# An mLSTM and window-attention decoder layer on one core: the first output gates beside the sample attention, sample states in half tiles, and other steps moved

## The chip, the cores and the metric

The kernel runs on one core of a Trainium2 chip. The metric is device time in microseconds (us), the median of several runs. A profiled execution gives the trace; its line numbers are those of the kernel before. Engines are called PE (TensorE, matrix products), DVE (VectorE), ACT (ScalarE), POOL (GpSimd) and SP (SyncE, which issues most of the DMAs from a queue in order).

## The reference

One layer of a hybrid decoder is applied to a prompt (512 tokens) and to 8 samples of 4 tokens, which come with a state. All data are float32.

```python
u = x @ w_in                                   # 2048 -> 18952 columns
q_m,k_m,v_m,o_m,z_m, q_a,k_a,v_a,z_a, g_m,g_a, i_pre,f_pre = split(u)
# mLSTM, 4 heads of 512; per chunk, with carry (C, n, m)
s    = (q @ k.T) * d                           # d: decays of the gates
num  = s @ v + inter * (q @ C);  den = sum(s) + inter * (q @ n)
h_m  = num / max(|den|, exp(-m_row))
C    = decay * C + (w * k).T @ v               # samples: C is (8, 4, 512, 512), read and written
# attention over a window of 128, 32 heads of 64, 4 kv heads, ALiBi, sinks
h_a  = softmax([q_a @ k_a.T / 8 - slope * dist, sink]) @ v_a
# merge
br_m = layernorm(h_m) * mlstm_norm_w * sigmoid(o_m) * silu(z_m)
br_a = h_a * silu(z_a)
y    = sigmoid(g_m) * (br_m @ w_proj_m) + sigmoid(g_a) * (br_a @ w_proj_a)
out  = layernorm(2**0.25 * x + y @ w_out)
```

It returns the outputs of prompt and samples, the mLSTM states C, n, m of both, and the last 128 keys and values of both.

## The kernel before

All 544 tokens (512 of the prompt, then 32 of the samples) go through one set of products. A float32 factor is split into a high part `wh` (rounded to the type of the fast product) and a rest `wl` (`split`, L177 to L184: a copy on ACT, a subtraction on DVE), and a product is the sum of three.

*First columns.* `gemm` multiplies the columns of the attention's values (two tiles of 128) and keys (two tiles) in the plain way, with `gates_product` after the first. `attn_values` and `attn_keys` transpose the results and store them. Beside them `x_sums` forms sums of quarters of x on POOL, DVE and ACT, which the next stage needs.

*Pairs.* `paired` goes over 72 pairs of 128 columns of `w_in`. By a scheme of Strassen's kind a pair is seven half products (`half_product`, L568 and L570, 24 matmuls of 272 columns each) instead of eight. `prepare` adds and splits weights up to three half products ahead, under a priority of `AHEAD` = 400; `gather` takes the results out of PSUM into the tiles O1 and O2 (pool `ev`, three buffers). At the end of a pair, `w["end"]` handles its two column tiles. The first 35 pairs (marked `acc`, they let a DMA do some of the additions) hold the 16 pairs of attention queries and their gates (`end_qz`), with other columns between. Then come, for the mLSTM heads 0 to 3, four pairs of output gates each (`end_oz`), heads 2 and 3 having six pairs of v, k and q ahead of theirs, and nine pairs of merge gates.

*Side work.* Generators in `live` are advanced by `tick()`, one step each; a pair calls it after the half products 0, 1, 3, 4 and 6. Two matter here. `attentions` does the prompt's attention for each pair of queries in 12 steps, then the attention of the samples (`sample_attention`), then opens the pools of the sample states (`open_samples`) and sets `state["samples"]`. `samples` takes mLSTM heads from `chain_` (a head enters when its last output-gate pair has ended) and runs `sample_head`: `sample_prep`, then for each of 8 batches a load of the state C (1 MB, `load_C`, L915), four or three steps, four matmuls with C (L1033), four updates (L1037, L1038) and two stores (L1040), then `sample_finish`. `until(cond)` calls `tick()` until a condition holds, with no product between; `end_qz(k)` uses it to let the attention of the pair before end, and `end_oz` to let the sample attention end:

```python
def end_oz(k):
    def end(o, z_):
        until(lambda: state["samples"])
        sg = st1([128, T], "sz", p="pz")
```

The tile `sz` comes from the pool `pz`, which `open_samples` opens.

*Order.* The program order gives each instruction a priority (a block under `tc.high_priority(offset=n)` counts as n instructions earlier). A scheduler in the framework then orders every engine's queue, DMA queues too, by these priorities and by its own model of the times, and sets all semaphores. On the chip each queue runs in that order. Tiles with the same tag in a pool share its buffers.

*Rest.* After the pairs, products with `w_proj_a`, beside the prompt's mLSTM cells, then with `w_proj_m` and `w_out`, and the layer norm.

The functions that the change touches, and those that call them:

Of the kernel before, what the change touches and what calls it, by code (L numbers as in the profile page):

```python
# [73 lines left out]
def _build(tc, nc, i, o, es):  # L74
# [123 lines left out]
    def mm():  # L198
        return psA.tile([128, 2, 512], F32, tag="mm", name=nm("mm"))

    def gemm(wv, c0, xh, xl, cols=EVEN, raws=(None, None), every=8):
        ps = mm()
        for half in range(2):
            raw = raws[half] or load_half(wv, c0, half)
            wh, wl = split(raw)
            products(ps, half, wh, wl, xh, xl, cols, every)
        return ps

# [271 lines left out]
    def last_sum(s4):  # L480

        for ch in range(4):
# [7 lines left out]
            hilo(r12, s4[0][:, ks_], s4[1][:, ks_])  # L490
            yield

    for kk in range(2):
        ps = gemm(win, VA_ + kk * 128, xh, xl, raws=((raw0[0], raw0[1]), (raw0[2], None))[kk], every=4)
        if kk == 0:
            spawn(x_sums())
            gates_ps = gates_product()
        vt = ev()
        A.copy(two(vt[:]), pv(ps))
        attn_values(kk, vt)  # L500
    for kk in range(2):
        ps = gemm(win, KA + kk * 128, xh, xl, every=4)
        kt = ev()
        A.copy(two(kt[:]), pv(ps))
        attn_keys(kk, kt)
    drain()
    for src, dst in ((d_ks, kb_s), (d_vr[SEQ:T], vb_s)):
        nc.sync.dma_start(dst[:, 124:128].rearrange("b t k d -> b t (k d)"), src.rearrange("(b t) c -> b t c", t=NTS))
# [93 lines left out]
    def paired(work, first=iter(())):  # L602

        steps = [(w, n) for w in work for n in range(7)]
        ready = 0
        load_a(work[0])
        load_b(work[0])
        for at, (w, n) in enumerate(steps):

            while ready < min(at + 3, len(steps)):  # L610
                with tc.high_priority(offset=AHEAD):
                    prepare(*steps[ready])
                ready += 1
            p = at // 7 + 1
            if p < len(work):
                if n == 3:
                    load_a(work[p])
                elif n == 4:
                    load_b(work[p])
            half_product(w, n)  # L620
            with tc.high_priority(offset=AHEAD):
                gather(w, n)
            next(first, None)
            if n == 6:
                w["end"](w["O1"], w["O2"])
            if n in (0, 1, 3, 4, 6):
                tick()


# [100 lines left out]
    def end_qz(k):  # L730

        def end(o1, o2):
            until(lambda: state["open"] and state["done"] == k)
            qs = []
            for a in range(2):
                q = btile("bq", [128, T], "q", F32R)
                own, oth = slice(a * 64, a * 64 + 64), slice(64 - a * 64, 128 - a * 64)
                A.activation(q[own], o1[own], AF.Copy, scale=-0.125)
                V.scalar_tensor_tensor(q[oth], o1[own], -0.125, r32(q[own]), op0=ALU.mult, op1=ALU.subtract)
                qs.append(q)  # L740
            nc.sync.dma_start(d_qa[k], o1[:, SEQ:T])
            sz = btile("b1", [128, T], "sz")
            A.activation(sz[:], o2[:], AF.Sigmoid)
            V.tensor_tensor(out=sz[:], in0=o2[:], in1=sz[:], op=ALU.mult)
            nc.sync.dma_start(d_bra[k][:, SEQ:T], sz[:, SEQ:T])
            waiting[k] = (qs, sz)
        return end

    def attentions():
        while gates_ in live:  # L750
            yield
        for _ in last:
            pass
        esG.close()
        open_attention()
        state["open"] = True
        for k in range(16):
            if k % 4 == 0:
                kv = kv_head(k // 4)
            while k not in waiting:  # L760
                yield
            yield
            yield from attention(k, *waiting.pop(k), kv)
            state["done"] = k + 1
        esB.close()
        yield from sample_attention()
        esT.close()
        open_samples()
        state["samples"] = True
# [2 lines left out]
    esT = ExitStack()  # L772

    def sample_attention():
        t1, t2 = pool(esT, "t1", 1), pool(esT, "t2", 2)
        gas = t1.tile([128, 16, NS], F32, name="gas")
        qraw = t1.tile([128, 2, GRP, NS], F32, name="qraw")
        qas = t1.tile([128, 2, NB, GRP, NTS], F32, name="qas")
# [72 lines left out]
        for b in range(NB):  # L851
            if b % 2 == 0:
                PTs = []
                for bb in range(2):
                    pt = sm()
                    PE.transpose(pt[:, 0:128], E[:, b + bb, 0:128], ident)
                    PE.transpose(pt[:32, 128:256], En[:, b + bb], ident)
                    PT = t2.tile([128, 256], F32, tag=f"PT{bb}", name=nm("PT"))
                    A.copy(PT[:, 0:128], pt[:, 0:128])
                    V.tensor_copy(PT[:32, 128:256], pt[:32, 128:256])  # L860
                    PTs.append(PT)
                yield
                yield
            PT = PTs[b % 2]
            for kvh in range(KVH):
                dst = po[(kvh % 2) * 64:(kvh % 2) * 64 + 64, (kvh // 2) * 256 + b * 32:(kvh // 2) * 256 + b * 32 + 32]
                tp = (0, (kvh % 2) * 64)
                PE.matmul(dst, vb[:, b, kvh * 64:kvh * 64 + 64], PT[:, kvh * 32:kvh * 32 + 32], start=True, stop=False, tile_position=tp)
                PE.matmul(dst, vas[:, kvh * 64:kvh * 64 + 64], PT[:32, 128 + kvh * 32:160 + kvh * 32], start=False, stop=True, tile_position=tp)
# [31 lines left out]
    sp = {}  # L901

    def open_samples():
        for name, bufs in (("s1p", 1), ("sC", 2), ("sw", 2), ("pz", 1)):
            sp[name] = pool(esS, name, bufs)

    def st1(shape, tag, dt=F32, p="s1p"):
# [3 lines left out]
        return sp["sw"].tile([128, 512], F32, tag="w", name=nm("w"))  # L911

    def load_C(h, b):
        ct = sp["sC"].tile([128, 4, 512], F32, tag="C", name=nm("C"))
        nc.sync.dma_start(ct[:], i["state_mlstm_C"][b, h].rearrange("(c p) v -> p c v", p=128))  # L915
        return ct

    def sample_prep(h, r):
        qs = st1([128, 4, NS], "qs", p="sw")
# [91 lines left out]
    def sample_head(h):  # L1011
        r = {}
        nxt = load_C(h, 0)
        yield from sample_prep(h, r)
        pC = None
        for b in range(NB):
            ct = nxt
            if b + 1 < NB:
                nxt = load_C(h, b + 1)

            qz = st1([128, 4, NS], "qz", p="sw")
            G.memset(qz[:], 0.0)
            G.tensor_copy(qz[:, :, b * 4:b * 4 + 4], r["qs"][:, :, b * 4:b * 4 + 4])
            Ab = st1([128, 512], "Ab", F32R)
            G.tensor_scalar(Ab[:], r32(r["kA"][:]), cc[:, C_M8 + b:C_M8 + b + 1], None, op0=ALU.mult)
            for _ in range(4 - b % 2):
                yield
            if b == 0:
                pC = sm()

            with tc.high_priority(offset=3000):
                for c in range(4):
                    PE.matmul(pC[c * 32:c * 32 + 32, :], qz[:, c], ct[:, c],  # L1033
                              start=(b == 0), stop=(b == NB - 1), tile_position=(0, c * 32))
            for c in range(4):
                pu = sm()
                PE.matmul(pu[:], Ab[:, c * 128:c * 128 + 128], r["V4"][:], start=True, stop=True)  # L1037
                V.scalar_tensor_tensor(ct[:, c], ct[:, c], dcb[:, h, b:b + 1], pu[:], op0=ALU.mult, op1=ALU.add)  # L1038
                if c % 2:
                    nc.sync.dma_start(C_s[b, h, (c - 1) * 128:c * 128 + 128, :].rearrange("(c p) v -> p c v", p=128),  # L1040
                                      ct[:, c - 1:c + 1])
        yield from sample_finish(h, r, pC)

    chain_ = []
# [1 line left out]

    def samples():
        while True:
            if not chain_:
                yield  # L1050
                continue
            h = chain_.pop(0)
            if h is None:
                break
            yield from sample_head(h)

        esS.close()
        pf = pool(esF, "pf", PF)
        for k in range(PF):
            st = pf.tile([128, T], F32, tag="pf", name=nm("pf"))  # L1060
            nc.sync.dma_start(st[:], d_bra[k])
            ahead.append(st)
# [10 lines left out]

    def end_oz(k):
        def end(o, z_):
            until(lambda: state["samples"])
            sg = st1([128, T], "sz", p="pz")
            A.activation(sg[:], z_[:], AF.Sigmoid)
            A.activation(o[:], o[:], AF.Sigmoid)
            V.scalar_tensor_tensor(sg[:], z_[:], wn[:, k:k + 1], sg[:], op0=ALU.mult, op1=ALU.mult)  # L1080
            G.tensor_tensor(out=sg[:], in0=sg[:], in1=o[:], op=ALU.mult)
            nc.sync.dma_start(d_g[k], sg[:])
# [38 lines left out]
            work.append(fill.pop(0))  # L1121
    for w in work:
        w["acc"] = True
    for h in range(MH):
        if h >= 2:
            work += vkq(h)
# [418 lines left out]
```

## Time and profile before

| | us |
|---|---|
| median of 3 runs | 2616.19 |
| lowest and highest | 2612.90, 2619.99 |
| the profiled execution | 2613.4 |
| its span in the trace | 2611.5 |
| PE busy | 2544.5 (97%) |
| DVE, ACT, POOL busy | 1694.6, 1178.1, 350.7 |
| mean granted clock of PE | 0.989 |

The trace covers 2611.5 of the profiled execution's 2613.4 us. The granted clock is 1.00 where PE runs at full speed. "A <- B" in a list of waits reads: A's engine sat idle before A until B had ended; a name with q (SPq) is an engine's queue of DMA issues. A matmul's duration is longer than the distance between the starts of two that follow each other, since they are pipelined.

### The profile page before, as it was taken

What the parts mean: (1) busy time and instruction counts of PE and PEld (TensorE: products, weight loads), DVE (VectorE), ACT (ScalarE), POOL (GpSimd) and SP (SyncE); (2) the same over time, 40 slices, a digit from 0 to 9 for tenths busy, and PEclk for the clock granted to TensorE, in tenths of its full rate; (3) what the DMA queues carried; (4) which work ended last, traced back from release to release, by engine and by line L of the source; (5) the groups of instructions that cost most, each with busy time, mean ns of one, the idle gap of its engine ahead of it and who ended that gap; (6) DMA issues with size and microseconds to landing.
All of it is one profiled execution on the core that took longest, in us unless ns stands there. A gap on an engine that the chain in (4) does not pass through costs nothing.

```text
span 2611.5 us, 48884 instructions
## 1 busy us (share of the span) xinstructions
PE 2544.5 (97%) x19970; PEld 2468.1 (95%) x19970; DVE 1694.6 (65%) x2508; ACT 1178.1 (45%) x1908; POOL 350.7 (13%) x334
## 2 busy tenths in 40 slices
PE   8999999999999998999999999999999999999997
PEld 7999999999999997989899899899999999999997
DVE  7867776676676673877778777776766553333336
ACT  4456676676676653434344334344633332222221
POOL 2111111111111101332123212210000000000002
PEclk9999999999999996999999999999999999999999
DMA  6576666666666653575774764774555545445432
GB/s 189 144 164 155 150 149 151 147 149 152 147 149 151 148 151 84 174 224 165 235 229 144 228 206 140 226 221 123 185 173 168 164 163 167 132 138 176 120 89 93
DMA packets 537103, 421.86 MB, mean 162 GB/s; under 512 B 43536, under 2 KB 449344, under 8 KB 536592
## 3 DMA queue, kind: packets, MB, share of 16 engines
q1 hardware_dynamic: 526800, 382.04, 48.6%
q0 software_dynamic: 10080, 36.70, 8.3%
q8 instruction: 157, 2.57, 0.4%
q14 instruction: 66, 0.54, 0.1%
HBM read 297.66 MB, written 86.42 MB: 147 GB/s over the span
## 4 chain that ended last, share of the span: by engine, by line
PE 79%; DVE 6%; DMA 5%; ACT 3%; issue 2%; POOL 0%; DVEq 0%; SPq 0%; ACTq 0%
PE mm L568 31%; PE mm L191 21%; PE mm L570 14%; DMA raw<-in_w_in 2%; PE sm L1208 2%; DMA C<-in_state_mlstm_C 2%; DVE wl L183 2%; PE sm L1240 1%; DMA out<-C 1%; ACT wh L182 1%; PE sm L1253 1%; DVE raw L545 1%; PE sm L714 1%; PE sm L1033 1%; PE sm L704 1%
## 5 line engine op out<-in xcount | busy, mean ns | idle before, releaser
L182 ACT CAST wh<-raw 128x1024 fp32r<-128x1024 f32 x604 | 632.9, 1048 | 989.3 <-PE mm L568 624.6
L183 DVE TENSOR_TENSOR wl<-raw,wh 128x1024 fp32r<-128x1024 f32 x604 | 749.8, 1245 | 424.2 <-ACT wh L182 394.6
L545 DVE TENSOR_TENSOR raw<-raw,raw 128x1024 f32<-128x1024 f32 x218 | 269.0, 1234 | 90.9 <-DMA raw<-in_w_in 81.9
L568 PE MATMUL mm<-xk,wh 128*128 128x272 f32 x2304 | 315.4, 289 | 4.9 <-DVE ev L594 3.1
L568 PEld LDWEIGHTS mm<-xk,wh 128*128 128x128 f32 x2304 | 298.8, 188 | 15.5 <-ACT ev L587 5.1
L191 PE MATMUL mm<-bl,wh 128*128 128x272 f32 x1024 | 213.9, 288 | 0.0
L191 PE MATMUL mm<-bh,wl 128*128 128x272 f32 x1024 | 213.8, 289 | 0.0
L191 PE MATMUL mm<-bh,wh 128*128 128x272 f32 x1024 | 213.5, 289 | 0.0
L570 PE MATMUL mm<-xk,wl 128*128 128x272 f32 x1152 | 170.7, 289 | 0.0
L191 PEld LDWEIGHTS mm<-bh,wh 128*128 128x128 f32 x1024 | 160.6, 188 | 1.5 <-issue 1.5
L191 PEld LDWEIGHTS mm<-bl,wh 128*128 128x128 f32 x1024 | 161.6, 188 | 0.0
L191 PEld LDWEIGHTS mm<-bh,wl 128*128 128x128 f32 x1024 | 160.7, 189 | 0.0
L570 PEld LDWEIGHTS mm<-xk,wl 128*128 128x128 f32 x1152 | 154.2, 189 | 6.8 <-issue 6.7
L568 PE MATMUL mm<-n2h,wh 128*128 128x272 f32 x576 | 153.2, 297 | 5.8 <-ACT wh L182 5.7
L588 POOL TENSOR_TENSOR ev<-p,ev 128x272 f32<-128x272 f32 x72 | 93.5, 1298 | 483.8 <-ACT ev L587 418.6
L568 PE MATMUL mm<-n3h,wh 128*128 128x272 f32 x576 | 150.1, 292 | 3.8 <-DVE ev L590 3.8
L568 PE MATMUL mm<-s4h,wh 128*128 128x272 f32 x576 | 149.5, 291 | 0.5 <-ACT ev L592 0.5
L568 PE MATMUL mm<-n3l,wh 128*128 128x272 f32 x576 | 149.4, 291 | 0.0
L568 PE MATMUL mm<-s1l,wh 128*128 128x272 f32 x576 | 148.9, 289 | 0.0
L568 PE MATMUL mm<-s1h,wh 128*128 128x272 f32 x576 | 148.7, 288 | 0.0
L568 PE MATMUL mm<-n2l,wh 128*128 128x272 f32 x576 | 148.2, 288 | 0.0
L568 PE MATMUL mm<-s4l,wh 128*128 128x272 f32 x576 | 147.9, 290 | 0.0
(425 smaller groups left out, 5510.5 us busy)
## 6 DMA issues: line engine op xcount, KB each, us to landing
raw<-in_w_in SPq DMA_DIRECT2D x296, 512.0 KB, 4.0
raw<-raw POOLq DMA_DIRECT2D x70, 512.0 KB, 5.3
C<-in_state_mlstm_C SPq DMA_DIRECT2D x32, 1024.0 KB, 5.8
out<-C SPq DMA_DIRECT2D x64, 512.0 KB, 5.8
raw<-in_w_proj_a SPq DMA_DIRECT2D x32, 512.0 KB, 4.1
raw<-in_w_proj_m SPq DMA_DIRECT2D x32, 512.0 KB
raw<-in_w_out SPq DMA_DIRECT2D x32, 512.0 KB, 4.0
d_sgm<-ev SPq DMA_DIRECT2D x16, 272.0 KB, 4.0
```

What stands on the lines that cost most here:

```text
L182: A.copy(wh[:], raw[:])
L183: V.tensor_tensor(out=wl[:], in0=raw[:], in1=r32(wh[:]), op=ALU.subtract)
L191: PE.matmul(ps[:, f, :w], a[:, kk], b(k, c, w), start=(k == 0 and n == 0), stop=(k == 15 and n == 2))
L545: V.tensor_tensor(out=w[out][:], in0=w[a][:], in1=w[b][:], op=ALU.add)
L568: PE.matmul(ps, wh[:, k], x(p, k), start=(first and k == 0 and p == 0), stop=False, skip_group_check=True)
L570: PE.matmul(ps, wl[:, k], x(0, k), start=False, stop=(k == 7), skip_group_check=True)
L588: G.tensor_tensor(out=c22, in0=p1, in1=c11, op=ALU.subtract)
L704: PE.transpose(pt[:, (m - m0_) * 128:(m - m0_) * 128 + 128], s_[:, b, 128:256] if own else s_[:, b + 1, 0:128], ident)
L714: PE.matmul(po[:, b * 128:b * 128 + n], VA[:, b], p_[:, 2 * b:2 * b + n // 128], start=(b == 0 and m == 0), stop=(b == 3 and m == 1), skip ...
L1033: PE.matmul(pC[c * 32:c * 32 + 32, :], qz[:, c], ct[:, c], start=(b == 0), stop=(b == NB - 1), tile_position=(0, c * 32))
L1208: PE.matmul(pp[:, 0:258], a[:, b * 128:b * 128 + 128], b_[:, b, f], start=(b == 0 and n == 0), stop=(b == 3 and n == 2))
L1240: PE.matmul(pp[:, 0:n], x_[c][:, b * 128:b * 128 + 128], y_[c][:, b * 128:SEQ], start=(c == 0 and m == 0), stop=(c == 3 and m == 2))
```

## The change

- `gemm` can split its weights under a priority, and does so for the second tile of values and both of keys (150); the gates' product, the evacuations and `attn_values`, `attn_keys` are put ahead by 150 too (`ahead_of_sums`).
- Pairs that are not marked `acc` call `tick()` after each of the seven half products, instead of five of them.
- `end_qz` splits the queries under the priority `AHEAD`.
- `end_oz` no longer waits for the sample attention. Its pool `pz` is opened before the prompt's attention, in the stack of the pairs. A head of `samples` now starts only when `state["samples"]` is set.
- In the sample attention the pool `t2` has one buffer, and the tiles `PT` lie by turns in it and in the tiles `kT`.
- A sample state is loaded in two half tiles of 512 KB, from four buffers instead of two whole ones.
- Every batch of `sample_head` has five steps before its matmuls, instead of four and three by turns.

```diff
-    def gemm(wv, c0, xh, xl, cols=EVEN, raws=(None, None), every=8):
+    def gemm(wv, c0, xh, xl, cols=EVEN, raws=(None, None), every=8, prio=0):
...
-            wh, wl = split(raw)
+            if prio:
+                with tc.high_priority(offset=prio):
+                    wh, wl = split(raw)
+            else:
+                wh, wl = split(raw)
...
+    def ahead_of_sums():
+        return tc.high_priority(offset=150)
+
     for kk in range(2):
-        ps = gemm(win, VA_ + kk * 128, xh, xl, raws=((raw0[0], raw0[1]), (raw0[2], None))[kk], every=4)
+        ps = gemm(win, VA_ + kk * 128, xh, xl, raws=((raw0[0], raw0[1]), (raw0[2], None))[kk], every=4, prio=150 * kk)
         if kk == 0:
             spawn(x_sums())
-            gates_ps = gates_product()
+            with ahead_of_sums():
+                gates_ps = gates_product()
         vt = ev()
-        A.copy(two(vt[:]), pv(ps))
-        attn_values(kk, vt)
+        with ahead_of_sums():
+            A.copy(two(vt[:]), pv(ps))
+            attn_values(kk, vt)
     for kk in range(2):
-        ps = gemm(win, KA + kk * 128, xh, xl, every=4)
+        ps = gemm(win, KA + kk * 128, xh, xl, every=4, prio=150)
         kt = ev()
-        A.copy(two(kt[:]), pv(ps))
-        attn_keys(kk, kt)
+        with ahead_of_sums():
+            A.copy(two(kt[:]), pv(ps))
+            attn_keys(kk, kt)
...
-            if n in (0, 1, 3, 4, 6):
+            if not w.get("acc") or n in (0, 1, 3, 4, 6):
                 tick()
...
         def end(o1, o2):
             until(lambda: state["open"] and state["done"] == k)
             qs = []
-            for a in range(2):
+            with tc.high_priority(offset=AHEAD):
+                for a in range(2):
...
         esG.close()
+        sp["pz"] = pool(esQ, "pz", 1)
         open_attention()
...
-        t1, t2 = pool(esT, "t1", 1), pool(esT, "t2", 2)
+        t1, t2 = pool(esT, "t1", 1), pool(esT, "t2", 1)
...
-                    PT = t2.tile([128, 256], F32, tag=f"PT{bb}", name=nm("PT"))
+                    p_, t_ = (t1, "kT") if b % 4 else (t2, "PT")
+                    PT = p_.tile([128, 2, 128], F32, tag=f"{t_}{bb}", name=nm("PT"))[:].rearrange("p a b -> p (a b)")
...
-        for name, bufs in (("s1p", 1), ("sC", 2), ("sw", 2), ("pz", 1)):
+        for name, bufs in (("s1p", 1), ("sC", 4), ("sw", 2)):
...
-        ct = sp["sC"].tile([128, 4, 512], F32, tag="C", name=nm("C"))
-        nc.sync.dma_start(ct[:], i["state_mlstm_C"][b, h].rearrange("(c p) v -> p c v", p=128))
-        return ct
+        out = []
+        for g in range(2):
+            ct = sp["sC"].tile([128, 2, 512], F32, tag="C", name=nm("C"))
+            nc.sync.dma_start(ct[:], i["state_mlstm_C"][b, h, g * 256:g * 256 + 256].rearrange("(c p) v -> p c v", p=128))
+            out += [ct[:, 0], ct[:, 1], ct]
+        return out[0:2] + out[3:5], (out[2], out[5])
...
-            for _ in range(4 - b % 2):
+            for _ in range(5):
                 yield
...
-            if not chain_:
+            if not chain_ or not state["samples"]:
                 yield
                 continue
...
         def end(o, z_):
-            until(lambda: state["samples"])
             sg = st1([128, T], "sz", p="pz")
```

More of the change, by code (lines that the diff above doesn't have):

```diff
@@ L734, in end @@
             qs = []
-            for a in range(2):
[L736 to L740, printed above, removed]
+            with tc.high_priority(offset=AHEAD):
+                for a in range(2):
+                    q = btile("bq", [128, T], "q", F32R)
+                    own, oth = slice(a * 64, a * 64 + 64), slice(64 - a * 64, 128 - a * 64)
+                    A.activation(q[own], o1[own], AF.Copy, scale=-0.125)
+                    V.scalar_tensor_tensor(q[oth], o1[own], -0.125, r32(q[own]), op0=ALU.mult, op1=ALU.subtract)
+                    qs.append(q)
             nc.sync.dma_start(d_qa[k], o1[:, SEQ:T])
@@ L1016, in sample_head @@
         for b in range(NB):
-            ct = nxt
+            ct, whole_ = nxt
             if b + 1 < NB:
@@ L1032, in sample_head @@
                 for c in range(4):
-                    PE.matmul(pC[c * 32:c * 32 + 32, :], qz[:, c], ct[:, c],
+                    PE.matmul(pC[c * 32:c * 32 + 32, :], qz[:, c], ct[c],
                               start=(b == 0), stop=(b == NB - 1), tile_position=(0, c * 32))
@@ L1037, in sample_head @@
                 PE.matmul(pu[:], Ab[:, c * 128:c * 128 + 128], r["V4"][:], start=True, stop=True)
-                V.scalar_tensor_tensor(ct[:, c], ct[:, c], dcb[:, h, b:b + 1], pu[:], op0=ALU.mult, op1=ALU.add)
+                V.scalar_tensor_tensor(ct[c], ct[c], dcb[:, h, b:b + 1], pu[:], op0=ALU.mult, op1=ALU.add)
                 if c % 2:
                     nc.sync.dma_start(C_s[b, h, (c - 1) * 128:c * 128 + 128, :].rearrange("(c p) v -> p c v", p=128),
-                                      ct[:, c - 1:c + 1])
+                                      whole_[c // 2][:])
         yield from sample_finish(h, r, pC)
```

## The prediction

> **What bounds the kernel now.** I read the head of the page first, then stretches of the span, then TensorE's timeline around the one bad slice, then the lists of waits.
>
> ```profile
> span 2611.5 us, 48884 instructions
> PE 2544.5 (97%) x19970; PEld 2468.1 (95%) x19970; DVE 1694.6 (65%) x2508; ACT 1178.1 (45%) x1908; POOL 350.7 (13%) x334
> PEclk9999999999999996999999999999999999999999
> ```
>
> TensorE (PE) is busy 97% of the span, so the kernel can only get shorter where PE waits or runs below full clock: 67 us of idling, and the one slice (the 16th, 65 us long) whose clock is 6 tenths. A view by stretches (us, then busy time of PE, its weight loads, DVE, ACT, POOL, the granted clock, DMA) and PE's timeline open that slice:
>
> ```profile
> 973.75:1017.45 43.70, 29.76 (x213) 21.97 (x212) 13.24 (x38) 11.89 (x39) 0.45 (x1) 0.57 0.01 3
> 976.40:985.36 8.96, 0.00 (x1) 0.00 (x1) 4.31 (x13) 5.05 (x20) 0.00 (x0) 0.68 0.00 0
> 985.36:1013.67 28.31, 27.23 (x144) 20.34 (x144) 2.86 (x14) 5.83 (x17) 0.00 (x0) 0.50 0.00 1
> 1017.45:1020.74 3.29, 3.29 (x14) 3.29 (x15) 0.00 (x0) 0.40 (x1) 1.91 (x4) 0.51 0.95 199
> ```
>
> ```profile
> 955.05 2.16 PE L568 MATMUL mm<-xk,wh 128*128 128x272 f32 x16
> 958.05 0.29 PE L568 MATMUL mm<-a11h,wh 128*128 128x272 f32 x1
> ...
> 964.93 0.60 PE L807 MATMUL sm<-cc,kb 128*128 128x128 f32 x4
> ...
> 973.25 0.50 PE L570 MATMUL mm<-xk,wl 128*128 128x272 f32 x2
> ...
> 975.95 0.42 PE L824 MATMUL sm<-kT,qas 64*32 64x128 f32 x8
> 985.36 0.48 PE L856 MATMUL sm<-cc,E 128*128 128x128 f32 x1 [8.99 <-ACT E L845]
> 985.63 0.42 PE L857 MATMUL sm<-cc,En 128*32 128x128 f32 x1
> 985.84 0.42 PE L856 MATMUL sm<-cc,E 128*128 128x128 f32 x1
> ...
> 1013.25 0.42 PE L869 MATMUL sm<-PT,vas 32*64 32x32 f32 x2
> 1017.45 0.60 PE L568 MATMUL mm<-n3h,wh 128*128 128x272 f32 x1 [3.79 <-DVE ev L590]
> ...
> 1020.74 0.29 PE L568 MATMUL mm<-n3h,wh 128*128 128x272 f32 x1
> ```
>
> From 973.75 to 1017.45 no half product (L568, L570) runs. This is the `until` of `end_oz`: the first output-gate pair may not end before the sample attention has, so its remaining steps run one behind the other: softmax with PE idle for 9 us, then 16 transposes and 128 small matmuls at half clock, then the wait for the evacuation. The rest of PE's waits, in us, times, longest:
>
> ```profile
> PE sm L856 <- ACT E L845: 9.0, 1, 9.0
> PE sm L676 <- DVE q L739: 8.4, 11, 0.8
> PE sm L1033 <- DMA C<-in_state_mlstm_C: 7.6, 7, 2.3
> ...
> PE mm L568 <- ACT wh L182: 5.7, 15, 1.7
> PE mm L568 <- DVE ev L590: 3.8, 1, 3.8
> ...
> PE sm L439 <- ACT ev L499: 2.6, 1, 2.6
> PE mm L191 <- DVE wl L183: 1.9, 2, 1.4
> ```
>
> **Part 1, output gates beside the sample attention.** The wait in `end_oz` goes, the tile of `pz` exists from the start of the prompt attention, and the heads wait for `state["samples"]` instead. Counting yields in the code, the sample attention has 28 steps (5+4+4+4+3+8). It begins at the end of the first gate pair (the 36th of 72). A half product is 3.00 us (955.05 to 958.05), a pair of seven 21 us. With a step behind each half product 28 steps last four pairs, 84 us: all four pairs of head 0 now lie beside it. What is recovered is the stall less the work that PE must do anyway:
> - the gap is 43.70 us, to which the restart at half clock adds 3.29 us where 14 half-product matmuls at (2.16 - 0.29)/15 = 0.125 us take 1.76: 1.5 lost;
> - what remains of keys and scores, to 976.4, costs 2.6 us at full clock, and stays;
> - the 144 instructions from 985.36 to 1013.67 keep PE busy for 27.23 us at clock 0.50. A transpose starts every 0.21 us there (985.63, 985.84), but every (0.60 - 0.29)/3 = 0.10 at full clock (964.93), so I take half: 13.6 us, which also stays.
>
> So 43.7 + 1.5 - 2.6 - 13.6 = 29.0 us. If the small matmuls (no row has them at full clock) did not gain from it, 27.2 would stay and 15.4 be won; I take 29.0, by the transposes. The cover for this work is the products of four pairs. ACT and DVE must then serve both:
>
> ```profile
> 1050.00:1750.00 700.00, 687.20 (x5268) 638.78 (x5267) 539.69 (x649) 279.41 (x348) 164.04 (x143) 1.00 0.65 200
> 1350.00:1400.00 50.00, 50.00 (x398) 48.34 (x397) 42.78 (x57) 25.57 (x34) 11.01 (x8) 1.00 0.52 155
> 1750.00:1800.00 50.00, 49.60 (x394) 49.16 (x393) 33.97 (x33) 21.91 (x27) 4.35 (x3) 1.00 0.49 145
> ```
>
> Pairs alone take 34 of 50 us of DVE (last row), so 57 of 84; with all of the gap's 13.24 on top it is 70 of 84 us, 84%, and the middle row has PE full beside a DVE at 86%. ACT changes its table whenever an Exp of the attention follows a Sigmoid of a gate:
>
> ```profile
> 979.77 1.28 ACT L836 ACT_TABLE_LOAD   x1 [3.88 <-DVE sast L834]
> ```
>
> Even two loads for each of four gates are 10 us, beside an ACT that is busy 22 of 50 us with pairs: nothing on the path. The attention's loads leave at the step where they left before; only the store of `gas` now has the weights of four pairs around it in SP's queue (a rival, below). PE takes its queue in order, though, so a score, transpose or value group that was queued a little too early stops the products: I put four such waits at the 0.8 us of L676, 3 us lost. The single buffer of `t2` costs nothing, since alternate groups of `PT` lie in the two dead `kT` tiles.
>
> **Part 2, queries split ahead.** The row of L676 is 8.4 us in 11 of 16 pairs. Its releaser stands behind a weight split on DVE:
>
> ```profile
> 911.39 1.21 DVE L183 TENSOR_TENSOR wl<-raw,wh 128x1024 fp32r<-128x1024 f32 x1
> 912.63 1.47 DVE L739 SCALAR_TENSOR_TENSOR q<-ev,q 64x544 fp32r<-64x544 f32 x2
> ```
>
> Ahead by 400, the queries (1.47 us of DVE) pass that split, which becomes later by this. Splits run up to three half products, 9 us, ahead, so that is covered; without cover it would be 1.5 us in 16 pairs, 24 us lost. I take 7 won of 0 to 8.4.
>
> **Part 3, states in half tiles, five even steps per batch.** Same bytes, 64 loads for 32.
>
> ```profile
> SPq L915 <- DMA out<-C: 83.3, 28, 5.7
> SPq L876 <- DVE gas L875: 46.0, 1, 46.0
> ```
>
> ```profile
> raw<-in_w_in SPq DMA_DIRECT2D x296, 512.0 KB, 4.0
> ...
> C<-in_state_mlstm_C SPq DMA_DIRECT2D x32, 1024.0 KB, 5.8
> out<-C SPq DMA_DIRECT2D x64, 512.0 KB, 5.8
> ```
>
> Today a state's load stands at the head of SP's queue until both stores of the old state have landed (3 us each time), with weight loads behind it, and PE waits 7.6 us for states. A half tile is free after its own store, and a batch comes every 5 steps (15 us) where it came after 4 or 3 uneven ones. A head has 6+40+2 = 48 steps at 7 a pair, 6.9 pairs (36 at 5, 7.2, before); head 0 starts one pair later, and head 3 still waits for its own gates: the end of the stage doesn't move. I take half of the 7.6, 4 won; the most is 7.6, and the loss is a rival below. The Trainium skill (DMA: Bandwidth & Descriptors, "Rules for kernel authors") speaks against halves: it asks for 1 MiB or more per DMA. The rows agree in direction (two transfers of 4.0 for one of 5.8); by that rule this part would win nothing, and the total would be 4 us higher.
>
> **Part 4, splits and evacuations ahead of the sums of x.**
>
> ```profile
> 39.90:56.00 16.10, 12.12 (x74) 11.84 (x74) 14.85 (x22) 7.11 (x15) 9.50 (x8) 0.79 0.51 138
> 45.00:51.00 6.00, 5.81 (x25) 5.81 (x26) 6.00 (x12) 1.94 (x3) 1.85 (x2) 0.50 0.83 224
> ```
>
> ```profile
> L568 PE MATMUL mm<-a11h,wh x576: 283/287/292, 89.0 to 1855.1; 128*128 128x272 f32 x192
> ```
>
> PE idles 4.0 us here (the waits of L439 and L191 above) and loses half of 5.8 us to the clock: 6.9 in all. DVE is busy 14.85 of 16.10, so what is put first makes the sums later, and the first pair (from 89.0) reads them. I take 4 won, between 6.9 and a loss of 4 (the idling returns there).
>
> **The sum.** 29 - 3 + 7 + 4 + 4 = 41 us off the profiled execution's 2613.4: 2572. That execution is 2.8 us below the median of the runs, 2616.2, so the forecast is 2575.
>
> **Rivals.**
> *The clock falls beside the products (0.14).* PE was busy for 27.23 of 28.31 us and yet stayed at 0.50, so small matmuls do not hold the clock. They come in four bursts of 32 (3.0 us each at 27.23/144/2). If each burst lets the clock fall, it takes 3.0 us more, and the return loses 1.6: 18 us in all, and the time is 2593. For: that row. Against: the half products on both sides had it back within 3.3 us. The Trainium skill (TensorE: Matmul & The Clock Gate, "What's actually happening") grants the full clock after some 3.4 us of busy PE. The row contradicts it for matmuls this small; by the rule this rival would be void and the 29 safe.
> *The stage stays serial (0.05).* The change would not do what it says if SP again holds the store of `gas` at its head (46.0 us above), now with the weights of four pairs behind it. Past the 9 us of split lead PE would stand, and 26 us of part 1 are gone: 2601. Against: the scheduler had nothing else to put there before.
> *Slower (0.11): the half loads block SP.* Each of the 32 added loads may stand at SP's head as today's do, 83.3/28 = 3.0 us, with weights behind it. It decides from 1.2 us passed on to PE per added load (32 x 1.2 = 38; the other parts win 37). At the full 3.0 it is 96 - 37 = 59 us slower, 2675. For: DMA carries 200 GB/s in that stage and PE already loses 12.8 us there. Against: each half waits for half the bytes, and 83.3 us of SP today cost PE only 7.6.
>
> **Numbers.** The forecast has 0.68; 0.02 is left for no change. A measurement of this kernel tells some 0.3% (7.8 us; the runs spread 7). Faster by more: 0.68 + 0.14 + 0.05 = 0.87; within: 0.02; slower: 0.11. The low end is the sum with parts 2 to 4 whole and no new waits (2575 - 1 - 4 - 3 - 3 = 2564), and 2 us of spread below it; the high end takes in the clock's case with part 4 won back (2593 + 8 = 2601). The forecast's own cases and the clock's hold 0.82.
>
> **What would show it.** Right: no slice with a low clock; the waits of L856 and of L590's reader gone; L868 between half products, at some 0.1 us each; no L676 in the list of waits; the last a11h product (1855.1) about 41 us earlier and the first (89.0) about 4. Wrong: a stretch of several us without L568 or L570 near 980; the clock below 1.00 there; more PE idling than 12.8 us in the head stage, with SP's waits for stores well above 83 us; a first pair that waits for the sums.

## The result, and the profile after

The changed kernel takes 2615.12 us (median of 12 runs, 2612.86 to 2622.01) where the kernel before takes 2615.43 (12 runs, 2612.9 to 2620.21). The ratio, estimated from all the runs and not from the two medians, is 1.0002, with a 95% interval of 0.9993 to 1.0012. Nothing is won, where 41 us were forecast. The profiled execution took 2615.85 us. The head of its page:

```profile
span 2614.1 us, 48916 instructions
PE 2560.7 (98%) x19970; PEld 2466.6 (94%) x19970; DVE 1699.9 (65%) x2508; ACT 1180.1 (45%) x1910; POOL 341.0 (13%) x334
PEclk9999999999999999999999999999999999999999
```

The slice with the low clock is gone and PE idles 53 us where it idled 67; yet PE's busy time is 16 us longer with the same 19970 matmuls. To see where, the span is cut at the starts of first products: of the first pair, of the second output-gate pair (the 37th of 72), of the 43rd pair (the last of head 1's output gates), and of the last pair. The three stretches are called the first stage, the gates stage and the head stage. The view by stretches, first of the kernel before:

```profile
89.04:958.05 869.01, 856.41 (x6807) 848.68 (x6806) 610.04 (x979) 559.01 (x1013) 123.29 (x122) 1.00 0.63 150
958.05:1129.27 171.22, 155.38 (x1230) 139.38 (x1229) 104.09 (x153) 68.36 (x113) 33.94 (x33) 0.88 0.52 153
1129.27:1853.35 724.08, 712.00 (x5483) 669.67 (x5482) 548.59 (x644) 293.89 (x365) 146.57 (x127) 1.00 0.62 190
```

and of the changed one:

```profile
86.53:956.46 869.93, 855.49 (x6807) 847.43 (x6806) 611.95 (x983) 563.16 (x1017) 123.84 (x125) 1.00 0.63 150
956.46:1092.68 136.22, 135.72 (x1153) 129.77 (x1152) 89.14 (x124) 64.39 (x110) 20.36 (x17) 0.97 0.46 129
1092.68:1855.85 763.17, 751.07 (x5561) 681.04 (x5559) 569.16 (x674) 295.70 (x367) 152.42 (x142) 1.00 0.62 191
```

The gates stage (second row) is 35.0 us shorter: Part 1 works there. The head stage (third row) is 39.1 us longer, all of it in busy time: 712.00 to 751.07, with idling at 12.1 in both. Some 77 matmuls of head 0 crossed from the one stage to the other, so the two must be read as a sum (+4.1); with 2.5 us won ahead of the first pair and 0.9 lost in the first stage this makes the 2.6 by which the span grew.

What became busier in the head stage is one group, the matmuls with the states. From the groups of instructions, before and after:

```profile
L1033 PE MATMUL sm<-C,qz 128*32 128x512 f32 x256 | 33.3, 603 | 7.6 <-DMA C<-in_state_mlstm_C 7.6
```
```profile
L1052 PE MATMUL sm<-C,qz 128*32 128x512 f32 x256 | 58.2, 603 | 6.4 <-DMA C<-in_state_mlstm_C 5.9
```

256 instructions of 603 ns on average in both, but they cover 33.3 us before and 58.2 us after. PE's timeline says why; one batch before, then one after:

```profile
1127.43 1.06 PE L1033 MATMUL sm<-C,qz 128*32 128x512 f32 x8
```
```profile
1146.16 1.05 PE L1052 MATMUL sm<-C,qz 128*32 128x512 f32 x4
...
1155.08 1.05 PE L1052 MATMUL sm<-C,qz 128*32 128x512 f32 x4
```

The four matmuls of a batch (two instructions each) are written with `tile_position=(0, c * 32)`: each uses 32 columns of the array. Eight instructions that stand together take 1.06 us, so they run side by side; four take 1.05 us all the same. With half tiles each pair of them waits for a load of its own, and in 24 of 32 batches the scheduler put products between the pairs (the first two batches of each head still stand together). Such a batch then costs 2.1 us for 1.06.

The lists of waits after, PE's rows and that of SP's queue:

```profile
PE sm L687 <- DVE q L751: 8.4, 11, 0.8
...
PE sm L1052 <- DMA C<-in_state_mlstm_C: 5.9, 10, 1.6
PE mm L579 <- ACT wh L182: 4.5, 10, 2.3
PE mm L323 <- DVE wga L318: 2.6, 1, 2.6
PE sm L425 <- ACT t L407: 1.9, 1, 1.9
...
PE mm L579 <- ACT p L590: 1.5, 1, 1.5
...
SPq L933 <- DMA out<-C: 195.0, 58, 6.0
```

The waits of L856 and of L590's reader (line numbers of the kernel before) are gone. The wait for the queries (L687, L676 before) is untouched. SP stands 195.0 us behind the stores of states, where it stood 83.3.

### The profile page after: what moved, and what is told of

It is laid out like the page before. It is cut to its first block, busy times and chain, and to the rows that moved or that the text cites. A ratio compares the mean times of both kernels' runs of the same rounds, so it can differ in the third digit from the quotient of the medians.

```text
span 2614.1 us, 48916 instructions
## 1 busy us (share of the span) xinstructions
PE 2560.7 (98%) x19970; PEld 2466.6 (94%) x19970; DVE 1699.9 (65%) x2508; ACT 1180.1 (45%) x1910; POOL 341.0 (13%) x334
## 4 chain that ended last, share of the span: by engine, by line
PE 80%; DVE 5%; DMA 5%; ACT 3%; issue 1%; SPq 0%; POOL 0%; DVEq 0%; ACTq 0%; POOLq 0%
PE mm L579 32%; PE mm L191 21%; PE mm L581 15%; DMA out<-C 2%; PE sm L1227 2%; DVE wl L183 2%; PE sm L1052 2%; DMA C<-in_state_mlstm_C 1%; DMA raw<-in_w_in 1%; PE sm L1259 1%; PE sm L1272 1%; ACT wh L182 1%; PE sm L725 1%; DVE raw L556 1%; PE sm L715 1%
## 5 line engine op out<-in xcount | busy, mean ns | idle before, releaser
L579 PEld LDWEIGHTS mm<-xk,wh 128*128 128x128 f32 x2304 | 299.5, 188 | 24.4 <-issue 13.8
L191 PE MATMUL mm<-bl,wh 128*128 128x272 f32 x1024 | 213.9, 288 | 0.0
L191 PE MATMUL mm<-bh,wl 128*128 128x272 f32 x1024 | 213.8, 289 | 0.0
L191 PE MATMUL mm<-bh,wh 128*128 128x272 f32 x1024 | 213.5, 289 | 0.0
L191 PEld LDWEIGHTS mm<-bh,wh 128*128 128x128 f32 x1024 | 160.6, 188 | 1.5 <-issue 1.5
L191 PEld LDWEIGHTS mm<-bl,wh 128*128 128x128 f32 x1024 | 161.6, 188 | 0.0
L191 PEld LDWEIGHTS mm<-bh,wl 128*128 128x128 f32 x1024 | 160.7, 189 | 0.0
L579 PE MATMUL mm<-a11h,wh 128*128 128x272 f32 x576 | 148.9, 290 | 0.0
L579 PE MATMUL mm<-a11l,wh 128*128 128x272 f32 x576 | 148.9, 291 | 0.0
```

The source lines that it names most:

```text
L191: PE.matmul(ps[:, f, :w], a[:, kk], b(k, c, w), start=(k == 0 and n == 0), stop=(k == 15 and n == 2))
L579: PE.matmul(ps, wh[:, k], x(p, k), start=(first and k == 0 and p == 0), stop=False, skip_group_check=True)
```

## The experiments

Theory after the result: the half tiles cost what Part 1 wins, through matmuls that no longer run side by side. Rivals: SP's queue, blocked more often by half loads; smaller transfers; the crowding of the side work. Ratios are to the kernel before on the same chip, with 95% intervals; "PE for states" and "SP for stores" are those lists of waits, in us.

| kernel | ratio | state matmuls, PE busy | PE for states | SP for stores |
|---|---|---|---|---|
| before | 1 | 33.3 | 7.6 | 83.3 |
| changed | 1.0002 [0.9993, 1.0012] | 58.2 | 5.9 | 195.0 |
| whole_states | 0.9941 [0.9926, 0.9955] | 33.3 | 9.0 | 79.0 |
| together | 1.0008 [0.9998, 1.0019] | 35.1 | 17.3 | 211.0 |
| halves_alone | 1.0087 [1.0072, 1.0102] | 58.2 | 6.7 | 184.7 |
| gates_alone | 0.9920 [0.9907, 0.9933] | 33.3 | 9.5 | 81.5 |
| steps_before | 0.9938 [0.9924, 0.9951] | 34.1 | 13.6 | 90.5 |
| attention_later | 0.9948 [0.9933, 0.9963] | 33.3 | 10.3 | 94.3 |
| sums_alone | 1.0001 [0.9991, 1.0011] | 33.3 | 8.3 | 86.3 |
| together_pool | 1.0069 [1.0056, 1.0082] | 37.5 | 33.3 | – |
| apart | 0.9987 [0.9977, 0.9996] | 64.2 | 1.7 | 75.5 |
| two_loads | 0.9941 [0.9928, 0.9954] | 33.4 | 12.0 | 81.6 |
| no_priority | 0.9893 [0.9879, 0.9908] | 41.2 | 1.1 | 90.6 |
| together_no_priority | 0.9992 [0.9982, 1.0002] | 37.0 | 7.4 | 214.5 |
| together_plain | 0.9994 [0.9984, 1.0005] | 34.7 | 17.8 | 216.5 |

**whole_states**: the change with whole states again.

```diff
-        for name, bufs in (("s1p", 1), ("sC", 4), ("sw", 2)):
+        for name, bufs in (("s1p", 1), ("sC", 2), ("sw", 2)):
...
-        for g in range(2):
-            ct = sp["sC"].tile([128, 2, 512], ...)
-            nc.sync.dma_start(ct[:], i["state_mlstm_C"][b, h, g * 256:g * 256 + 256]...)
+        ct = sp["sC"].tile([128, 4, 512], ...)
+        nc.sync.dma_start(ct[:], i["state_mlstm_C"][b, h]...)
...
```

> The changed kernel, but with whole states of 1 MB from two buffers. Theory 1 (columns): the four matmuls of a batch with C use four column strips of the array side by side, and where the halves are issued apart each pair costs what four cost together; without halves the 25 us of PE time that L1052 gained over L1033 (58.2 against 33.3) go: 2590 us, PE busy in the state matmuls back to 33. Theory 2 (SP): the halves cost because their loads block SP's queue (195 us against 83): 2590 too, with SP's waits for stores back near 83. Theory 3 (steps): the head stage is longer because of the steps behind every half product and the five steps per batch, not the halves: 2615.

Measured 0.9941, and 33.3 us for the state matmuls. Undoing the halves wins 16 us (0.0061 of 2615). This refutes theory 3; theories 1 and 2 had expected 25 us, so the busy time came back whole and the time only for two thirds.

**together**: half tiles, but the four matmuls of a batch follow each other in the queue.

```diff
-                for c in range(4):
-                    PE.matmul(pC[c * 32:c * 32 + 32, :], qz[:, c], ct[c], ...)
...
+                state_product(2)
+                last_ = state_product(3)
+                with tc.issue_after(getattr(last_, "ins", last_)):
+                    state_product(0)
+                    state_product(1)
```

> The changed kernel with its half tiles, but the two matmuls of the first half are issued directly behind those of the second half, so that all four stand next to each other in PE's queue. Theory 1: 2590 us, state matmuls at 33 us of PE, though SP still waits some 190 us for stores. Theory 2: 2615, since the transfers are unchanged. Theory 3: 2615.

Measured 1.0008. The busy time came back (35.1), and the time did not: the waits took its place (17.3 for states), and PE's idling in the head stage rose from 12.1 to 28.4 us. Theory 1 alone (2590 us) fails here. Its head stage:

```profile
1098.03:1858.29 760.26, 731.86 (x5560) 681.20 (x5559) 565.03 (x674) 294.82 (x367) 162.52 (x142) 0.99 0.64 192
```

**halves_alone**: the kernel before with half tiles and nothing else (the same diff as whole_states, the other way).

> The kernel before with half tiles (four buffers) and nothing else. Theories 1 and 2: 2640 us (25 more), state matmuls at 58 us of PE. Theory 3: 2615.

Measured 1.0087, 23 us slower. Its head stage is 750.2 us for 724.1; PE is busier there by 22.6 of these 26.1 us. The half tiles of Part 3 by themselves lose what Part 1 wins.

```profile
1134.06:1884.29 750.23, 734.58 (x5484) 673.36 (x5482) 550.85 (x645) 294.87 (x366) 139.35 (x126) 1.00 0.61 183
```

**gates_alone**: whole_states without Part 4 and without the priority of the queries; Part 1 and the even steps remain.

```diff
-        return tc.high_priority(offset=150)
+        return ExitStack()
...
-            with tc.high_priority(offset=AHEAD):
+            with ExitStack():
```
(`prio=` is left out of the calls of `gemm`, too.)

> Part 1 alone with its steps: the gates beside the sample attention, a step behind every half product, five steps per batch, whole states, no queries ahead, no priority over the sums of x. By the starts of the pairs in the two traces part 4 won 0.9 us net and part 2 nothing: 2591 us by theories 1 and 2, within 2 us of whole_states; 2616 by theory 3.

Measured 0.9920, 21 us faster (17.6 to 24.4). Its gates and head stages:

```profile
958.84:1092.17 133.33, 132.73 (x1152) 126.81 (x1151) 88.32 (x122) 64.38 (x110) 19.31 (x17) 1.00 0.49 132
1092.17:1837.94 745.77, 724.98 (x5560) 675.15 (x5559) 564.43 (x674) 294.26 (x367) 164.12 (x142) 1.00 0.64 196
```

Together 879.1 us for 895.3 before. Parts 2 and 4 add nothing that is seen here; that whole_states lies 0.0021 higher isn't explained (the intervals overlap).

**steps_before**: gates_alone with the old steps behind the sample attention.

```diff
-            if not w.get("acc") or n in (0, 1, 3, 4, 6):
+            if (not w.get("acc") and not state["samples"]) or n in (0, 1, 3, 4, 6):
...
-            for _ in range(5):
+            for _ in range(4 - b % 2):
```

> gates_alone, but once the sample attention has ended the pairs call tick() after five of seven half products again and the batches have four and three steps by turns: the head stage goes as in the kernel before, with whole states. In gates_alone the stages of gates and heads together won 16.5 us in the trace where part 1 was forecast at 26; the head stage shows 6 to 9 us more PE idling than before. Theory A (steps): the even steps cost this; ratio to the kernel before 0.988 (2590 where before is 2620), PE idling in the head stage back to some 12 us. Theory B (crowding): the idling comes from head work that now lies in fewer pairs, whatever the steps: ratio 0.992 as gates_alone.

Measured 0.9938, where theory A had 0.988: the even steps are not what eats Part 1; if anything they help (waits for states 9.5 against 13.6; the intervals overlap).

**attention_later**: gates_alone with one more `yield` ahead of each prompt attention, to give the queries time.

> gates_alone, but the prompt's attention for a pair of queries starts one step (one half product, 3 us) later. Putting the queries' split ahead leaves every queue in the same order, since the chain from the last evacuation over the ACT copy to the DVE subtraction takes 2 us whatever its priority, and PE comes to the scores 1.2 us after that evacuation. Theory: the 8.4 us of waits for q go, ratio 0.989 (3 thousandths below gates_alone). Rival: the extra step is drained in end_qz without a product between, and the 8 us come back there: ratio 0.992.

Measured 0.9948, no gain. The wait that it was to remove stands in the list of PE's waits to the digit:

```profile
PE sm L687 <- DVE q L751: 8.4, 11, 0.8
```

In this trace and in that of gates_alone the scores that wait stand directly behind the same half product (a11h). The extra step did not move them, so the run leaves open what later scores would win.

**sums_alone**: the kernel before with Part 4 alone (the diff of `gemm`, `ahead_of_sums` and its uses).

> The kernel before with part 4 alone (splits and evacuations ahead of the sums of x). By the pair starts of the traces: first pair 2.4 us earlier, sixth 2.8 later (whole_states) or 0.9 earlier (the changed kernel). Theory: the sums come back as waits of the first pairs, ratio 1.000 to 1.002. Rival (the forecast): 4 us won, ratio 0.9985.

Measured 1.0001: Part 4 is worth nothing.

**together_pool**: together, with the half loads in POOL's queue, where no weights stand behind them.

```diff
-            nc.sync.dma_start(ct[:], i["state_mlstm_C"][b, h, g * 256:g * 256 + 256]...)
+            nc.gpsimd.dma_start(ct[:], i["state_mlstm_C"][b, h, g * 256:g * 256 + 256]...)
```

> together (half tiles, four state matmuls side by side), but the loads of the half states go from POOL's queue, so that SP and the weights behind it no longer wait for the stores of old states. Theory 2 (SP): in together the 17.3 us that PE waits for states and the 9.3 for L605 come from SP's 211 us at the head of its queue; here they fall to some 8 and 4: ratio 0.994 where together had 1.0008. Rival (transfers): the halves land late because of DMA time or of where the scheduler puts the matmuls: 1.000.

Measured 1.0069, slower than either theory had it. POOL's queue stands behind stores as SP's did, and PE waits longer for states:

```profile
POOL C L933 <- DMA out<-C: 107.9, 24, 15.7
PE sm L1052 <- DMA C<-in_state_mlstm_C: 33.3, 16, 4.9
```

So this run does not tell a blocked SP from a crowded DMA.

**apart**: gates_alone, whole states, with the last two of the four matmuls a step later.

```diff
-            with tc.high_priority(offset=3000):
-                for c in range(4):
-                    PE.matmul(pC[c * 32:c * 32 + 32, :], qz[:, c], ct[c], ...)
+            for cs_ in ((0, 1), (2, 3)):
+                with tc.high_priority(offset=3000 if cs_[0] == 0 else 1):
+                    for c in cs_:
+                        PE.matmul(pC[c * 32:c * 32 + 32, :], qz[:, c], ct[c], ...)
+                if cs_[0] == 0:
+                    yield
```
(and four steps ahead of them instead of five.)

> gates_alone (whole states, one load each), but the matmuls with the second half of a state are issued after another step and without priority, so that the four of a batch never stand together in PE's queue. Columns theory: state matmuls at 58 to 67 us of PE where gates_alone has 33.3, and the time 25 us above gates_alone: ratio 1.001 to 1.002. Rival (the halves cost through their transfers alone): ratio 0.992.

Measured 0.9987 against 0.9920: 17.5 us lost with no half tile in the kernel. Its group and its head stage:

```profile
L1050 PE MATMUL sm<-C,qz 128*32 128x512 f32 x256 | 64.2, 605 | 1.7 <-DMA C<-in_state_mlstm_C 1.7
...
1089.96:1851.44 761.48, 755.80 (x5560) 678.90 (x5559) 563.71 (x674) 294.87 (x367) 154.62 (x142) 1.00 0.63 192
```

PE is 30.8 us busier than in gates_alone and idles 15.1 less (5.7 for 20.8). That matmuls apart cost double is shown, and also that about half of this cost fills time in which PE would have waited.

**two_loads**: gates_alone with each whole tile filled by two loads of 512 KB, the matmuls side by side, the tile still freed as a whole.

```diff
-        nc.sync.dma_start(ct[:], i["state_mlstm_C"][b, h]...)
+        for g in range(2):
+            nc.sync.dma_start(ct[:, g * 2:g * 2 + 2], i["state_mlstm_C"][b, h, g * 256:g * 256 + 256]...)
```
(The four matmuls are written as in together, the second half first.)

> gates_alone with whole state tiles that are freed whole, but each filled by two loads of 512 KB; the four matmuls stay side by side. If the size of a transfer costs (two shorter DMAs for one of 1 MB): PE's waits for states near together's 17 us, ratio 1.000. If it costs that a half's load waits at SP's head for its own store: as gates_alone, 0.992.

Measured 0.9941 against 0.9920, with intervals that overlap: two transfers for one cost some 5 us, or nothing.

**no_priority**: gates_alone without the priority of the state matmuls.

```diff
-            with tc.high_priority(offset=3000):
+            with ExitStack():
                 for c in range(4):
```

> gates_alone without the priority of 3000 on the state matmuls: they stand where their step is, five steps after the load's issue, and not where the scheduler believes that the load has landed. Theory (placement): PE's waits for states (9.5 us) go, since the loads land earlier than the step: ratio 0.9885. Rival: later matmuls mean later stores and later loads, and the waits stay or move to other tiles: 0.992 or more.

Measured 0.9893, the fastest version here, 28 us below the kernel before. The group in its trace:

```profile
L1049 PE MATMUL sm<-C,qz 128*32 128x512 f32 x256 | 41.2, 605 | 1.2 <-DMA C<-in_state_mlstm_C 1.1
...
1093.03:1838.38 745.35, 733.15 (x5560) 676.40 (x5559) 563.90 (x674) 292.80 (x367) 162.96 (x142) 1.00 0.65 196
```

The waits for states fall from 9.5 to 1.1 and PE idles 12.2 us for 20.8, but some batches lie apart now and PE is 8.2 us busier. In the traces the two head stages are equally long; the 7 us between the two kernels are not located (this profiled execution was the slowest of the kernel's four runs), and the two intervals touch.

**together_no_priority**: the same edit on together.

> together (half tiles, side by side) without that priority. Together paid 17 us of waits for states. Placement theory: these are PE reaching the matmuls before the second half has landed, and go: ratio 0.993 (with parts 2 and 4 as in the changed kernel). Rival: the transfers of halves cost in themselves, 1.000.

Measured 0.9992, no different from together beyond the intervals. The waits for states fall from 17.3 to 7.4 us, and PE's wait for DVE's evacuations (L605) rises from 7.3 to 19.0: SP stands 214.5 us behind stores, and PE idles 30.7 us in the head stage.

**together_plain**: together without Part 4. It differs from two_loads in the tiles (two per state, each freed by its own store) and in that it keeps Part 2. The latter changes nothing: in the two traces PE, DVE and ACT do the same instructions in the same order up to 1130 us, past the last queries.

> together without part 4: it differs from two_loads (0.9941) only in that a state lies in two tiles, so that each half is freed, and its load stands at SP's head for its own store, by itself. If freeing by halves costs (SP at its head for stores some 210 us instead of 82, weights late): ratio 0.999 to 1.001 and waits of DVE for weights near together's 73 us. If it does not, and together differed by part 4: 0.994 and 62 us.

Measured 0.9994 against 0.9941 of two_loads: 14 us, with the intervals well apart. Waits and head stage of two_loads:

```profile
PE sm L1050 <- DMA C<-in_state_mlstm_C: 12.0, 10, 2.5
SPq L932 <- DMA out<-C: 81.6, 28, 5.9
DVE raw L556 <- DMA raw<-in_w_in: 61.7, 27, 5.8
...
1094.04:1845.69 751.65, 728.23 (x5561) 678.51 (x5559) 565.00 (x674) 294.51 (x367) 162.91 (x142) 1.00 0.64 194
```

and of together_plain (the row of DVE in both is that of the head stage alone):

```profile
PE sm L1052 <- DMA C<-in_state_mlstm_C: 17.8, 14, 3.1
SPq L933 <- DMA out<-C: 216.5, 58, 6.6
DVE raw L556 <- DMA raw<-in_w_in: 81.6, 28, 5.6
...
1092.82:1859.63 766.81, 733.16 (x5560) 681.24 (x5559) 565.65 (x674) 294.36 (x367) 158.81 (x142) 0.99 0.63 190
```

The same bytes move in transfers of the same size. What differs is that SP now stops 58 times instead of 28, 135 us more, with weights behind it. DVE waits 20 us more for weights, PE 6 more for states, and PE idles 33.7 us in the stage for 23.4.

## Why the prediction was wrong

**The account.** The forecast was 26 us won by Part 1, 7 by Part 2, 4 by Part 3 and 4 by Part 4. By the runs, Part 1 with even steps wins 21 us (gates_alone), the half tiles lose 23 (halves_alone), and Parts 2 and 4 win nothing that is seen. These pieces add up to 2 us lost, and none was measured.

**Part 3 is the step that failed.** It was entered as 4 us won, and it loses 16 (whole_states) to 23 (halves_alone). I costed the loads and never the four matmuls that read them; the sum had no term for these. Two things were missing:
- The matmuls cost 1.06 us together and 2.1 us apart (above). This is 24.9 us of busy PE, and apart shows it without any half tile. The Trainium skill (TensorEngine Tiling (Array Packing), "Key Properties") states that different tiles can load weights and multiply in parallel, independently; the trace agrees, 8 instructions in 1.06 us. A split into two waits puts this sharing at risk, and the row with x256 that shows it was in the trace of the kernel before.
- Freeing by halves makes SP stop twice as often: 14 us in together_plain against two_loads. This is the mechanism of the rival "slower", which I gave 0.11. My argument against it, that a half tile waits for half the bytes, was wrong: the wait per stop did not halve (81.6/28 = 2.9 us, 216.5/58 = 3.7).

In the changed kernel the two do not add: matmuls apart fill time in which PE would have waited (idling is 12.1 us; put together, 28.4). That is why together, which removes the first, gains nothing. The rule of the Trainium skill that the prediction cited against halves, 1 MiB or more per DMA (DMA: Bandwidth & Descriptors, "Rules for kernel authors"), named the smaller cost: two_loads puts it at some 5 us, or nothing.

**Part 1 held in its place and was too large.** Forecast 26 us; 21 by runs of gates_alone, 16.2 in its trace. There PE's idling in the gates stage fell by 15.2 us (13.9 forecast, the 43.70 less 29.76 of the gap), and its busy time in the gates and head stages together by 9.7 where 15.1 were forecast. Of the 5.4 missing, 2.8 are the small matmuls: two start every 0.23 us at full clock, 0.115 each, where I took half of their 0.19 at half clock, by the transposes. The other 2.6 are not located. From PE's timeline of the changed kernel:

```profile
1009.36 0.30 PE L884 MATMUL sm<-PT,vas 32*64 32x32 f32 x2
1009.59 0.30 PE L883 MATMUL sm<-PT,vb 128*64 128x32 f32 x2
1009.82 0.30 PE L884 MATMUL sm<-PT,vas 32*64 32x32 f32 x2
```

The rest of the loss is idling: in the head stage of gates_alone PE idles 8.7 us more (20.8 for 12.1). The waits of the head stage, before:

```profile
PE sm L1033 <- DMA C<-in_state_mlstm_C: 5.9, 6, 2.3
PE mm L568 <- DVE ev L594: 2.7, 4, 0.8
DVE raw L545 <- DMA raw<-in_w_in: 47.6, 26, 4.4
```

and in gates_alone:

```profile
PE sm L1049 <- DMA C<-in_state_mlstm_C: 9.5, 9, 2.1
PE mm L579 <- DVE ev L605: 6.6, 6, 2.2
DVE raw L556 <- DMA raw<-in_w_in: 58.3, 26, 5.3
```

PE waits 3.6 us more for states (1.7 of them lay in the gates stage before, with the first batches of head 0) and 3.9 more for DVE's evacuations, and DVE waits 10.7 more for weights. The forecast "the end of the stage doesn't move" had no term for that; the 3 us for waits in PE's queue were meant for the gates stage, where none was needed (0.6 us of idling in 133).

**Part 2 did nothing.** The engines' queues have the same order with and without that priority (together_plain and two_loads, above). Both the split and the queries are put ahead by 400, and when the split is placed the queries are not ready: the last evacuation ends after the split's start. From DVE's timeline, with ACT's between:

```profile
909.45 0.44 DVE L609 SCALAR_TENSOR_TENSOR ev<-mm,p 128x272 f32<-128x272 f32 x1
909.80 1.22 DVE L183 TENSOR_TENSOR wl<-raw,wh 128x1024 fp32r<-128x1024 f32 x1
909.92 1.34 ACT L750 ACTIVATE q<-ev 64x544 fp32r<-64x544 f32 x2 [1.34 <-DVE ev L609]
911.05 1.47 DVE L751 SCALAR_TENSOR_TENSOR q<-ev,q 64x544 fp32r<-64x544 f32 x2
911.91 0.70 PE L687 MATMUL sm<-k,q 128*128 128x128 f32 x4 [0.76 <-DVE q L751]
```

The subtraction needs ACT's copy, and that needs L609, which runs just ahead of the split. The step "the queries pass that split" was read off the order on DVE without asking what the passing instruction waits for. That "the change doesn't do what it says" was a rival for Part 1 only; it belonged here.

**Part 4** started the first pair 2.5 us earlier (4 forecast). The waits that it was to remove went (L439 whole, L191 from 1.9 to 0.4 us), but ahead of the first pair PE now waits 2.6 us for the weights of the gates' product (L323 in the list above). New waits of the first pairs (L425 and L590, 3.4 us) then make the first stage 0.9 us longer. The prediction had named a return of the idling in the first pair as the lower end of this part. The sums of x that it feared for do end 2 to 4 us later, but no wait in the list names them. In sums_alone nothing is left of the gain.

**The clock rival** came partly true in the changed kernel. Stretches of 5 us there:

```profile
1035.00:1040.00 5.00, 5.00 (x40) 4.36 (x40) 2.13 (x3) 2.01 (x5) 0.68 (x1) 0.92 0.54 161
1040.00:1045.00 5.00, 5.00 (x32) 5.00 (x32) 1.05 (x4) 1.23 (x2) 0.00 (x0) 0.74 0.01 2
1065.00:1070.00 5.00, 5.00 (x31) 4.63 (x30) 2.39 (x9) 0.00 (x0) 1.56 (x3) 0.66 0.54 164
```

Two dips behind bursts of small matmuls, with PE busy throughout, cost some 3.4 us (0.08, 0.26 and 0.34 of 5 us) of the 18 feared. In whole_states PE's queue has the same order up to 1095 us, and its clock in that stage is 1.00. no_priority has gates_alone's order there, and 0.97 where gates_alone has 1.00 (135.82 us for 133.33). What decides whether a burst loses the clock is not shown.

**What was to show it.** No low slice, L856 gone, the small matmuls (L868 before, L883 now) between products: right. L676 gone, the last a11h product 41 us earlier: wrong (L676 is L687 now, 8.4 us as before, and that product comes 2.5 us later, at 1857.6). SP's waits "well above 83 us" were listed as the sign of a wrong prediction, and came.

**Open**: whether the 14 us of freeing by halves come through SP's queue alone or also through stores and loads that meet in the DMA engines; where no_priority gains its 7 us; the 0.0021 between whole_states and gates_alone.

## What to carry to other kernels

Before a tile is split, look at who reads it: if its readers share the array by `tile_position`, they must stay adjacent in PE's queue, and a second wait between them can cost as much as they do. Where loads wait for a buffer at the head of a queue that runs in order, count the stops: here twice as many stops for half the bytes each cost more, not the same. Before giving an instruction a priority, follow its own inputs: it passes nothing that starts before they are ready.

## What was not expected of the hardware

Two matmuls of 32 columns each (four instructions) took 1.05 us, and four (eight instructions) that stood together took 1.06; nothing in their mean duration (603 ns in both kernels) shows it, only the covered time does (33.3 and 58.2 us). PE can lose its granted clock to 0.74 and 0.66 while it shows 5.00 of 5.00 us busy. The Trainium skill (TensorE: Matmul & The Clock Gate, "What's actually happening") ties the full clock to some 3.4 us of busy PE; those two rows do not fit it for stretches with small matmuls.
